# New durations in the mixer's planner, and a rule for TensorE: six projection products before a turn to small ones

## The chip, the cores and the metric

The kernel runs on one core of a Trainium2 chip. Its engines work side by side, each through a list of instructions in a fixed order: TensorE (PE) multiplies matrices, VectorE (DVE) and ScalarE (ACT) do elementwise work and reductions, GpSimd (POOL) does elementwise work and indirect transfers, and SyncE (SP) issues most transfers. Where one engine needs what another makes, it waits for a semaphore. The metric is the device time of one launch in microseconds (us); lower is better.

## The reference, cut to what matters

One residual block of 512 tokens and 1024 features: a LayerNorm, a token mixer, a second LayerNorm, a mixture of 32 experts and a third LayerNorm. The change touches the token mixer.

```python
h = LayerNorm_in(x)
p = h @ W_in + b_in                       # columns: u, v | q, k, v | z | a, b | gates A, B
A = gMLP spatial gating(u, v)             # 8 groups of 128 channels, blocks of 128 positions
B = gated delta rule(q, k, v, a, b)       # 8 heads, 128 x 128 state, chunked along the tokens
m = (sigmoid(gA) * (A @ W_pa) + sigmoid(gB) * (B @ W_pb)) @ W_o
h = LN1(alpha * h + m)
out = LN2(alpha * h + HierMoE(h))         # each token goes to 2 of 32 experts
...
# one head of B: a causal convolution of 4 taps and SiLU on q, k, v; q and k scaled to length 1
lmat = where(strict, beta * (k @ k.T) * decay, 0)
sol  = triangular_solve(eye + lmat, [v * beta, k * beta * exp(G)])
for chunk in chunks:                      # the state goes from chunk to chunk
    v_new = u_c - w_c @ state
    o     = q_dec @ state + (q @ k.T * decay) @ v_new
    state = state * cd + k_dec.T @ v_new
B = o * rsqrt(mean(o * o)) * norm_w * silu(z)
```

## The kernel before

The tokens stand in four tiles of 128. A projection of 128 output features over all 512 tokens (`proj`) is 24 products of 128x512 on TensorE: for each of eight slices of the 1024 input features three products, since weights and activations are split into a high and a low part of the type float32r (`mm3`, `split`). The weights of one projection, 512 KB, are loaded by SP (`chunk`, `column`); ACT then makes `hi` and DVE makes `lo`. There are two buffers of `hi` and `lo`, and two PSUM buffers `pd` that the projections write to in turn.

The mixer is recorded first and issued later. `Rec` takes the place of the engines: each call, `rec.tensor.matmul(...)` for instance, becomes an `Op` with the engine, the operands, a `rank` and a cost. `Rec.order` then plays the engines through in a list schedule: it takes the engine that can start something first, and on it the ready operation of lowest rank (that recorded first, where ranks are equal). The order that comes out is the order of the instructions on every engine, since they are issued in it under a manual schedule. `Rec.cost` gives two numbers in ns: how long the engine is taken, and how long after that (before) the result is there for others. Nothing at run time changes this order; where the estimates are off, an engine waits at the instruction that the plan has put next.

The recording is issued in three parts (`rec.emit`): first the first LayerNorm (`norm_in`), the gMLP and the decays; then the heads; then the merge with the residual. Behind these the second LayerNorm, the router and the experts stand in orders of their own, which `Rec` does not touch.

In the heads' part each head `h` has a front and a chain:

- `front(h)`, of rank 2h, projects k, q and v (rank one higher), convolves them on ACT and DVE (`conv`), transposes k (`tr4`), takes ACT's sums of squares (`sumsq`, tile `junk`), forms k times k (`pkk`), decays it to `L`, inverts blocks of 8 on DVE (`pl`, `Lb`, `U8`), writes `U` and `Uc` and transposes `Uc` to `Tc` (`pu`), then transposes q, takes its sums of squares, multiplies k with q (`paq`), and transposes v. All its small products go through one PSUM buffer with the tag `pf`, one after the other; the chain's last step, `po`, uses it too. The trace calls the tiles of this buffer `pk`.
- `chain(h)`, of rank 2h+1, doubles the inverted blocks in steps from 8 to 128 (`pz`, `pt`, `pu`, masks from DVE in between), then goes through four chunks of 128 tokens: `p1` (state times k and q), `R`, `p2`, `V`, `p4` and the new state `Sn`, `p3` and `o`. At the end it norms `o`, projects z, transposes `o` (`po`) and splits the product to `yh` and `yl`. Its products of blocks use a part of the array only (`128*32`, `128*64`, `64*64` in the trace).

The chain of head h and the front of head h+1 are recorded side by side, so the projections of the next head lie between the small products of this one. The gates' projections (`gates_b`) fill up: two before the first chain, six beside the last. The merge's first projection (`psi<-yh,hi` in the trace) multiplies all heads' `yh` and `yl`, the last head's at the end.

In the trace, projection products read `hi` or `lo` and write `psi`; all recorded operations have the line L215, where `issue` gives them out, so they are told apart by their tiles.

Of the kernel before, what the change touches and what calls it, by code (L numbers as in the profile page):

```python
# [16 lines left out]
F32 = mybir.dt.float32  # L17
F32R = mybir.dt.float32r
# [4 lines left out]
OP = mybir.AluOpType  # L23
# [3 lines left out]
DRAM = bass.MemoryType.DRAM  # L27
# [51 lines left out]
class Rec:  # L79
# [12 lines left out]
    def add(self, attr, eng, name, args, kw):  # L92
        op = Op(eng, name, args, kw)
        op.attr, op.rank = attr, self.rank
        op.after = self.after if eng in self.after_on else None
        aps = [(k not in self.OUTS and not (i == 0 and "out" not in kw), x)
               for i, (k, x) in enumerate([(None, x) for x in args] + list(kw.items()))
               if isinstance(x, (bass.AP, Lazy))]
        op.uses = [(read, x.tensor.name) + self.hull(x) for read, x in aps]
        op.out = [x for read, x in aps if not read][0]  # L100
        self.psum.update(x.tensor.name for _, x in aps if isinstance(x, bass.AP) and x.space == PSUM)
        op.cost, op.late = self.cost(op)
        self.ops.append(op)
        return op
# [10 lines left out]
    def cost(self, op):  # L115

        n = 1
        for x in list(op.args) + list(op.kw.values()):
            if isinstance(x, (bass.AP, Lazy)):
                m = 1  # L120
                for d in list(x.ap)[1:]:
                    m *= d[1]
                n = max(n, m)
        if op.name == "dma_start":
            return (1300, 2600) if op.eng == "SP" else (500, 15000 if op.rank else 5000)
        if op.eng == "PE":
            if op.name == "transpose":
                return 110, 200
            rhs = op.args[2]
            n = 1  # L130
            for d in list(rhs.ap)[1:]:
                n *= d[1]
            if rhs.dtype in (F32R, BF):
                return 233, 20
            m = op.args[1].shape[-1]
            if m < 128:
                return (0.55 if m == 32 else 0.9) * n, 200
            return max(224, 1.75 * n), 200
        if op.eng == "DVE":
            if op.name == "tensor_reduce":  # L140
                return 150 + 2.0 * n, 33
            if op.name == "bn_stats":
                return 640, 33
            if n == 256 and len(op.out.shape) == 4 and op.out.shape[-1] == 8:
                return 1270, 33
            if op.name == "tensor_scalar" and n == 128 and op.out.dtype == F32 and isinstance(op.args[2], bass.AP):
                return 390, 33
            return 150 + (1.15 if op.name in ("scalar_tensor_tensor", "tensor_sub") else 1.06) * n, 33
        if op.eng == "ACT":
            if op.name == "activation" and n == 128 and isinstance(op.kw.get("scale"), bass.AP):  # L150
                return 405, 33
            return (485 if "accum_out" in op.kw else 170 + 0.87 * n), 33
        return (1010 if n < 16 else 250 + 2.25 * n), 33

    def order(self):
        ops = self.ops
        last = {}
        for i, op in enumerate(ops):
            op.i, op.deps, op.outs = i, set() if op.after is None else {op.after.i}, []
            for read, name, a, b in op.uses:  # L160
                log = last.setdefault(name, [])
                for j, r, a2, b2 in log:
                    if j != i and (a < b2 and a2 < b and not (read and r) or
                                   name in self.psum and "PE" not in (op.eng, ops[j].eng) and op.eng != ops[j].eng):
                        op.deps.add(j)
                if not read:
                    log[:] = [e for e in log if not (a <= e[2] and e[3] <= b) or e[0] == i]
                log.append((i, read, a, b))
            for j in op.deps:
                ops[j].outs.append(i)  # L170
        need = [len(op.deps) for op in ops]
        ready = [0.0] * len(ops)
        free = {}
        waiting = {}
        for op in ops:
            free.setdefault(op.eng, 0.0)
            waiting.setdefault(op.eng, [])
            if not need[op.i]:
                waiting[op.eng].append(op)
        out = []  # L180
        while len(out) < len(ops):
            best = None
            for e, w in waiting.items():
                if w:
                    t = max(free[e], min(ready[o.i] for o in w))
                    if best is None or t < best[0]:
                        best = t, e
            t, e = best
            w = waiting[e]
            op = min((o for o in w if ready[o.i] <= t), key=lambda o: (o.rank, o.i))  # L190
            w.remove(op)
            op.t = t
            free[e] = t + op.cost
            out.append(op)
            for j in op.outs:
                o = ops[j]
                lat = op.late
                if op.name != "dma_start":
                    lat = 0 if o.eng == e else max(lat, 150) if o.eng == "PE" else lat
                ready[j] = max(ready[j], t + op.cost + lat)  # L200
                need[j] -= 1
                if not need[j]:
                    waiting[o.eng].append(o)
        return out
# [1781 lines left out]
```

## Time and profile before

| | |
|---|---|
| median of the runs | 1206.45 us (1206.35 to 1207.39) |
| the profiled execution | 1204.72 us |
| its span, from the first to the last instruction | 1202.9 us |
| PE busy | 1045.7 us (87% of the span), 6866 products |
| DVE busy | 656.7 us (55%) |
| ACT busy | 401.1 us (33%) |
| POOL busy | 230.7 us (19%) |
| mean granted clock of TensorE | 0.938 |

Busy times are sums over stages with different limits. The mixer takes the first part of the span; in the experts' part the weights of the experts, 1024 KB for each load, take the DMA engines. The ends of TensorE's products are modelled in the profile, so consecutive products overlap in it; the distance from start to start is what one costs. A releaser in brackets (`<-ACT junk`) names the engine and tile whose semaphore ended an idle time.

### The profile page before, as it was taken

The page shows a single profiled execution, that of the slowest core. Times are in us where ns is not written, and L with a number is a line of the kernel's source. Part 1 is how long each engine was busy: PE and PEld are TensorE (multiplying, and loading weights), DVE is VectorE, ACT ScalarE, POOL GpSimd, SP SyncE. Part 2 cuts the span into 40 slices and gives each one's busy share as a digit, 9 for nine tenths or more (in the row PEclk, how much of TensorE's full clock was granted, in tenths as well). Part 3 has the DMA queues.
Part 4 walks back from the last instruction along what each step waited for, and adds up shares of the span by engine and source line. Part 5 has one row for each costly group of instructions (what it writes and reads, how often), then busy time and mean ns, then how long its engine had stood idle before and what let it go on. Part 6 is the DMA issues. An engine that isn't in the chain of part 4 may idle for free. (4 is left out here: it accounts for less than half of the span.)

```text
span 1202.9 us, 18914 instructions
## 1 busy us (share of the span) xinstructions
PE 1045.7 (87%) x6866; PEld 687.0 (57%) x6866; DVE 656.7 (55%) x1392; ACT 401.1 (33%) x849; POOL 230.7 (19%) x296
## 2 busy tenths in 40 slices
PE   3999999999999999999999968888888879767853
PEld 2788688867777777767788633443443334333321
DVE  7566535367586777764485645453333323335584
ACT  6333337335545445444533121121111101122210
POOL 1000100022212322230100123232222212233301
PEclk8999999999999999999999979999989989876767
DMA  4422342621122111111647579999999999987996
GB/s 174 162 70 72 119 144 88 214 84 53 54 70 71 53 53 54 53 54 61 223 159 297 210 287 385 387 401 397 393 399 399 380 408 413 409 328 302 409 407 241
DMA packets 57930, 268.82 MB, mean 223 GB/s; under 512 B 12881, under 2 KB 17265, under 8 KB 33736
## 3 DMA queue, kind: packets, MB, share of 16 engines
q1 hardware_dynamic: 44400, 246.96, 53.8%
q0 software_dynamic: 10224, 10.88, 3.0%
q10 hardware_dynamic: 3176, 9.20, 2.1%
q8 instruction: 87, 1.43, 0.5%
q14 instruction: 43, 0.35, 0.1%
HBM read 274.23 MB, written 27.29 MB: 251 GB/s over the span
## 5 line engine op out<-in xcount | busy, mean ns | idle before, releaser
L215 PE MATMUL psi<-hTh,lo 128*128 128x512 f32 x448 | 183.7, 411 | 1.6 <-DVE lo L215 1.6
L215 PE MATMUL psi<-hTh,hi 128*128 128x512 f32 x448 | 184.2, 414 | 0.9 <-ACT hi L215 0.5
L215 PE MATMUL psi<-hTl,hi 128*128 128x512 f32 x448 | 183.9, 413 | 0.0
L1547 DVE TENSOR_TENSOR h<-h,u 128x640 f32<-128x640 f32 x32 | 26.3, 821 | 245.4 <-ACT h L1546 245.4
L215 DVE TENSOR_TENSOR lo<-raw,hi 128x1024 fp32r<-128x1024 f32 x74 | 92.4, 1249 | 79.8 <-ACT hi L215 79.6
L215 ACT CAST hi<-raw 128x1024 fp32r<-128x1024 f32 x74 | 77.4, 1046 | 108.0 <-PE psi L215 91.1
L1539 PE MATMUL u<-raw,xs 128*32 128x256 f32 x1120 | 79.9, 427 | 30.4 <-DMA raw<-in_w 28.7
L215 PEld LDWEIGHTS psi<-hTh,lo 128*128 128x128 f32 x448 | 84.9, 190 | 21.4 <-issue 3.9
L215 PEld LDWEIGHTS psi<-hTh,hi 128*128 128x128 f32 x448 | 85.1, 190 | 20.2 <-issue 2.6
L215 PEld LDWEIGHTS psi<-hTl,hi 128*128 128x128 f32 x448 | 84.7, 189 | 17.5 <-issue 2.0
L1546 ACT ACTIVATE h<-u 128x640 f32<-128x640 f32 x32 | 22.5, 704 | 200.8 <-PEq L1481 151.9
L1539 PE MATMUL u<-raw,x 128*64 128x512 f32 x352 | 80.8, 608 | 2.5 <-PEq L1479 1.4
L1539 PEld LDWEIGHTS u<-raw,xs 128*32 128x32 f32 x1120 | 37.9, 120 | 65.7 <-DMA raw<-in_w 37.6
L1574 POOL DMA_INDIRECT y_rows<-ysmall,itail x28 | 26.1, 933 | 223.1 <-DVE ysmall L1594 205.9
L1556 ACT COPY hT<-t 128x128 f32<-128x128 f32 x32 | 8.5, 266 | 176.4 <-PE t L1553 176.4
L1574 POOL DMA_INDIRECT y_rows<-ylarge,islot x56 | 57.2, 1022 | 44.4 <-ACT ylarge L1599 31.0
L215 DVE SCALAR_TENSOR_TENSOR acc<-xp,cols,acc 128x512 f32<-128x512 f32 x72 | 54.5, 758 | 5.3 <-ACT acc L215 4.1
L1567 PE MATMUL yz<-raw,hT 128*32 128x256 f32 x560 | 44.7, 459 | 14.3 <-DMA raw<-in_w 5.5
L1539 PEld LDWEIGHTS u<-raw,x 128*64 128x64 f32 x352 | 28.4, 140 | 49.3 <-issue 46.2
L1594 DVE COPY ysmall<-yz 32x256 f32<-32x256 f32 x112 | 46.7, 417 | 6.6 <-PE yz L1567 4.1
L1567 PE MATMUL y<-raw,hT 128*64 128x512 f32 x168 | 39.0, 604 | 7.2 <-PEq L1479 6.9
L1514 PE MATMUL t<-ident,mh 64*128 64x64 f32 x256 | 24.4, 243 | 23.5 <-PEq L1481 19.1
(505 smaller groups left out, 1987.6 us busy)
## 6 DMA issues: line engine op xcount, KB each, us to landing
raw<-in_w SPq DMA_DIRECT2D x144, 1024.0 KB
raw<-in_wt SPq DMA_DIRECT2D x73, 512.0 KB
rawl<-in_w SPq DMA_DIRECT2D x24, 1024.0 KB
rawh<-in_w SPq DMA_DIRECT2D x24, 1024.0 KB
raw<-in_wv SPq DMA_DIRECT2D x8, 512.0 KB
y_rows<-zero SPq DMA_DIRECT2D x8, 512.0 KB
raw<-y_rows ACTq DMA_DIRECT2D x4, 1024.0 KB
rawl<-in_wo SPq DMA_DIRECT2D x3, 1024.0 KB
```

The costliest lines, as they stand in the source:

```text
L215: op._ins = getattr(getattr(self.nc, op.attr), op.name)(*map(real, op.args), **{k: real(x) for k, x in op.kw.items()})
L1514: nc.tensor.transpose(self.t[0][:, k * NA:k * NA + NA], r[0][:, k * 128:k * 128 + 128], ident[0:NA, 0:NA])
L1539: self.nc.tensor.matmul(self.u[q * r:(q + 1) * r, NP if p is None else p, 0:c], x[:, k, r0:r0 + r], self.raw[b, k // 2][:, o:o + c], start ...
L1546: self.nc.scalar.activation(out=h, in_=u[:, :, 0], func=AF.Silu)
L1547: self.nc.vector.tensor_mul(out=h, in0=h, in1=u[:, :, 1])
L1556: self.nc.scalar.copy(out=x[:, n], in_=self.t[1][:, 0:128])
L1567: self.nc.tensor.matmul(y[q * r:(q + 1) * r, 0:c], t[:, i, j * r:(j + 1) * r], self.raw[b, 4 + k // 2][:, o:o + c], start=k == 0, stop=k == 3)
L1574: x = self.nc.gpsimd.indirect_dma_start(out=out, out_offset=bass.IndirectOffsetOnAxis(ap=idx, axis=0), in_=src, in_offset=None, bounds_che ...
L1594: nc.vector.tensor_copy(out=small[:, q], in_=src)
```

## The change

The diff does three things, all in `Rec`.

1. `cost` gets a new table. For DVE, ACT and POOL it gives the time for which the engine is taken and the time from the start to the result, apart from each other; a small POOL operation that is no power falls from 1010 ns to 205, a product of 128x128 is put at 180 ns taken and 386 to its result, one in 32 columns at 60 and 300, and a projection product at 232 and 394 (233 and 20 behind that, before). A transfer's time from its issue to its landing stays the same sum.
2. `order` counts a result's time from the start of its operation, with 60 ns more if another engine uses it, and 30 ns more on the same engine, where a TensorE operation follows its predecessor at once.
3. On TensorE, `order` tells projection products (`wide`, operands of type float32r) from all others. It stays with the kind that it is at, as long as one of that kind is ready; from projection products it may turn to the others once six in a row are out, and then it stays with these until none is ready. Each turn is charged in the plan, 80 ns to the small ones and 120 ns back.

No operation is added or taken away, and no buffer, rank or transfer is changed.

```diff
--- before.py
+++ after.py
@@ -99,6 +99,7 @@
         op.uses = [(read, x.tensor.name) + self.hull(x) for read, x in aps]
         op.out = [x for read, x in aps if not read][0]
         self.psum.update(x.tensor.name for _, x in aps if isinstance(x, bass.AP) and x.space == PSUM)
+        op.wide = False
         op.cost, op.late = self.cost(op)
         self.ops.append(op)
         return op
@@ -122,35 +123,44 @@
                     m *= d[1]
                 n = max(n, m)
         if op.name == "dma_start":
-            return (1300, 2600) if op.eng == "SP" else (500, 15000 if op.rank else 5000)
+            return (1300, 3900) if op.eng == "SP" else (500, 15500 if op.rank else 5500)
+        column = any(isinstance(x, bass.AP) and x.space != DRAM and x.shape[-1] == 1
+                     for x in list(op.args[2:]) + [op.kw.get(k) for k in ("bias", "scale")])
         if op.eng == "PE":
             if op.name == "transpose":
-                return 110, 200
-            rhs = op.args[2]
+                return (109, 273) if op.args[1].shape[0] == 128 else (65, 216)
+            rhs, m = op.args[2], op.args[1].shape[-1]
             n = 1
             for d in list(rhs.ap)[1:]:
                 n *= d[1]
+            op.wide = rhs.dtype == F32R
             if rhs.dtype in (F32R, BF):
-                return 233, 20
-            m = op.args[1].shape[-1]
+                return 232, 394
             if m < 128:
-                return (0.55 if m == 32 else 0.9) * n, 200
-            return max(224, 1.75 * n), 200
+                return (max(60, 0.45 * n), 300) if m == 32 else (112, 278)
+            return max(180, 0.95 * n), max(386, 2.3 * n)
         if op.eng == "DVE":
             if op.name == "tensor_reduce":
-                return 150 + 2.0 * n, 33
-            if op.name == "bn_stats":
-                return 640, 33
-            if n == 256 and len(op.out.shape) == 4 and op.out.shape[-1] == 8:
-                return 1270, 33
-            if op.name == "tensor_scalar" and n == 128 and op.out.dtype == F32 and isinstance(op.args[2], bass.AP):
-                return 390, 33
-            return 150 + (1.15 if op.name in ("scalar_tensor_tensor", "tensor_sub") else 1.06) * n, 33
+                d = 145 + 2.0 * n
+            elif op.name == "bn_stats":
+                d = 684
+            elif op.name == "tensor_scalar" and n == 128 and op.out.dtype == F32 and column:
+                d = 400
+            elif op.name == "scalar_tensor_tensor":
+                d = 185 + 1.1 * n
+            else:
+                d = 145 + 1.06 * n
+            return max(60, d - 85), d
         if op.eng == "ACT":
-            if op.name == "activation" and n == 128 and isinstance(op.kw.get("scale"), bass.AP):
-                return 405, 33
-            return (485 if "accum_out" in op.kw else 170 + 0.87 * n), 33
-        return (1010 if n < 16 else 250 + 2.25 * n), 33
+            if "accum_out" in op.kw:
+                return 400, 430
+            d = 150 + 0.875 * n + (85 if column else 0)
+            return d - 85, d
+        if n < 16:
+            d = 1010 if any(x is OP.pow for x in op.kw.values()) else 205
+        else:
+            d = 200 + (0.7 if op.name == "tensor_copy" else 1.85) * n
+        return d + 80, d
 
     def order(self):
         ops = self.ops
@@ -177,7 +187,7 @@
             waiting.setdefault(op.eng, [])
             if not need[op.i]:
                 waiting[op.eng].append(op)
-        out = []
+        out, wide, run = [], None, 0
         while len(out) < len(ops):
             best = None
             for e, w in waiting.items():
@@ -187,17 +197,27 @@
                         best = t, e
             t, e = best
             w = waiting[e]
-            op = min((o for o in w if ready[o.i] <= t), key=lambda o: (o.rank, o.i))
+            some = [o for o in w if ready[o.i] <= t]
+            if e == "PE":
+                stay = [o for o in some if o.wide == wide]
+                if stay and (not wide or run < 6):
+                    some = stay
+            op = min(some, key=lambda o: (o.rank, o.i))
             w.remove(op)
+            if e == "PE":
+                if op.wide != wide and wide is not None:
+                    t += 120 if op.wide else 80
+                wide, run = op.wide, run + 1 if op.wide == wide else 1
             op.t = t
             free[e] = t + op.cost
             out.append(op)
             for j in op.outs:
                 o = ops[j]
-                lat = op.late
-                if op.name != "dma_start":
-                    lat = 0 if o.eng == e else max(lat, 150) if o.eng == "PE" else lat
-                ready[j] = max(ready[j], t + op.cost + lat)
+                if op.name == "dma_start" or o.eng != e:
+                    lat = op.late + (0 if op.name == "dma_start" else 60)
+                else:
+                    lat = op.cost if e == "PE" else op.late + 30
+                ready[j] = max(ready[j], t + lat)
                 need[j] -= 1
                 if not need[j]:
                     waiting[o.eng].append(o)
```

## The prediction

> **What bounds the kernel now.** I read the span first, then the busy time by stage, then who waited for whom on TensorE (PE), then TensorE's own order at two places. The change acts only on the mixer, whose order a planner in the kernel writes out; so the question is what TensorE loses there.
>
> ```profile
> span 1202.9 us, 18914 instructions
> ```
>
> The table by stage has the columns stretch, length, then busy us (and instructions) of PE, PE's weight load, DVE, ACT, POOL, the granted clock, the DMA share and GB/s.
>
> ```profile
> 0.00:36.00 36.00, 17.28 (x52) 11.32 (x53) 26.75 (x78) 23.84 (x39) 4.17 (x17) 0.81 0.54 193
> 36.00:236.00 200.00, 199.35 (x912) 159.35 (x911) 101.92 (x183) 80.74 (x143) 8.26 (x17) 1.00 0.35 114
> 236.00:520.00 284.00, 277.46 (x1696) 208.49 (x1694) 202.98 (x454) 139.26 (x375) 70.78 (x109) 1.00 0.20 63
> 520.00:560.00 40.00, 37.53 (x221) 27.20 (x222) 23.98 (x60) 15.15 (x43) 7.79 (x10) 0.96 0.17 53
> 560.00:676.00 116.00, 114.39 (x541) 91.01 (x540) 74.38 (x131) 45.50 (x64) 8.37 (x8) 1.00 0.52 192
> 676.00:1202.90 526.90, 399.70 (x3449) 189.60 (x3447) 226.65 (x490) 96.62 (x190) 131.34 (x135) 0.87 0.95 373
> ```
>
> Up to 676 us TensorE is the bound: it stands idle for 0.65 us between 36 and 236, for 6.5 us between 236 and 520 (the eight heads' chains), for 2.5 us up to 560, and for 1.6 us up to 676. Behind that the experts' weights bound the kernel (DMA share 0.95). Their stream begins when the mixer's memory is given back, so a mixer that ends earlier moves the rest with it; I take that at one to one. In the first 36 us TensorE idles 18.7 us, because the first LayerNorm feeds it.
>
> Busy time is not work, though. A batch that waits for its neighbour spreads out without showing as idle. The waits of PE between 236 and 572 us (total, times, longest):
>
> ```profile
> PE pk L215 <- ACT junk L215: 3.2, 12, 0.5
> PE psi L215 <- DVE lo L215: 1.6, 3, 1.2
> PE p L215 <- ACT V L215: 1.2, 2, 1.0
> ```
>
> **The change part by part.** First I need the price of a small product. In these rows of TensorE's order (start, modelled duration), `psi` are projection products of 512 columns and `pk`, `pt` are small ones; one fp32 product makes two records, a transposition makes one.
>
> ```profile
> 341.23 0.40 PE L215 MATMUL psi<-hTh,lo 128*128 128x512 f32 x1
> 341.46 0.39 PE L215 MATMUL psi<-hTl,hi 128*128 128x512 f32 x1
> 341.69 0.27 PE L215 MATMUL pk<-ident,qT 128*128 128x128 f32 x1
> 341.72 0.48 PE L215 MATMUL psi<-hTh,hi 128*128 128x512 f32 x1
> 342.04 0.39 PE L215 MATMUL psi<-hTh,lo 128*128 128x512 f32 x1
> ...
> 343.13 0.47 PE L215 MATMUL psi<-hTh,hi 128*128 128x512 f32 x1
> 343.44 0.38 PE L215 MATMUL pk<-qT,kT 128*128 128x128 f32 x2
> 343.58 0.48 PE L215 MATMUL psi<-hTh,lo 128*128 128x512 f32 x1
> 343.90 0.40 PE L215 MATMUL psi<-hTl,hi 128*128 128x512 f32 x1
> 344.23 0.43 PE L215 MATMUL pt<-Z,Tc 128*32 128x128 f32 x8
> 344.58 0.50 PE L215 MATMUL psi<-hTh,hi 128*128 128x512 f32 x1
> 344.92 0.39 PE L215 MATMUL psi<-hTh,lo 128*128 128x512 f32 x1
> ```
>
> Two projection products in a row start 0.23 us apart (341.23, 341.46). With one transposition between them, 341.46 to 342.04 is 0.58, which is two projections and 0.11. With one product between, 343.13 to 343.58 is 0.45, which is one projection and 0.22. So turning to a full-array small product and back costs only the product. A batch of eight records of the 32-column form costs more: 343.90 to 344.92 is 1.02, less two projections 0.55. The changed planner charges 0.08 and 0.12 us for every turn, and fewer turns would seem a gain by themselves; by these rows they are none for full-array products. I put the saving by fewer turns at 0.
>
> *The batch that gets entangled.* The four products of `kT` with `qT` (`paq`) share their PSUM buffer with the four sums of squares that ACT takes of q (`junk`). One head's pass:
>
> ```profile
> 388.54 0.40 PE L215 MATMUL psi<-hTh,lo 128*128 128x512 f32 x1
> 388.77 0.38 PE L215 MATMUL pk<-qT,kT 128*128 128x128 f32 x2
> 388.91 0.48 PE L215 MATMUL psi<-hTl,hi 128*128 128x512 f32 x1
> 389.61 0.49 PE L215 MATMUL pk<-qT,kT 128*128 128x128 f32 x2 [0.22 <-ACT junk L215]
> 389.94 0.27 PE L215 MATMUL pt<-ident,Uc 128*128 128x128 f32 x1
> 389.96 0.48 PE L215 MATMUL psi<-hTh,hi 128*128 128x512 f32 x1
> 390.56 0.49 PE L215 MATMUL pk<-qT,kT 128*128 128x128 f32 x2
> 390.98 0.41 PE L215 MATMUL pz<-U,B 128*32 128x128 f32 x2
> 391.31 0.49 PE L215 MATMUL pk<-qT,kT 128*128 128x128 f32 x2
> 391.73 0.42 PE L215 MATMUL pz<-U,B 128*32 128x128 f32 x6
> 392.08 0.50 PE L215 MATMUL psi<-hTh,lo 128*128 128x512 f32 x1
> ```
>
> From 388.54 to 392.08 is 3.54 us for three projections, four `paq`, one transposition and eight tiled records. Unentangled that is 3 x 0.23 + 4 x 0.22 + 0.11 + 0.55 = 2.23, so 1.3 us is lost. The new rule sends TensorE off for six projections (6 x 0.23 = 1.4 us) after the transposition that feeds the sums of squares. In the new cost table the four sums take 4 x 0.40; at the next turn at least three of them, and by the end of the third `paq` the fourth, are done, so that the four products go out together. Twelve waits at two a head are six heads: 6 x 1.3 = 7.8 us. Bounds: 0, if ACT is late and they stay entangled; 10.4, if all eight heads have it. I take 7.8, since the wait row is of this very thing.
>
> *Tiled batches cut in two.* Here `pz` went out as 2 and 6 records, at 0.33 (390.98 to 391.31) and 0.35: a part costs about as much as a whole, 0.33 extra. Going through TensorE's order I count seven cut batches, two of which lie inside the passes above. "Does all ready ones" comes behind a longer run, when the whole batch is ready more often. Five x 0.33 = 1.7; bounds 0 and 1.7; I take half, 0.8.
>
> *Other waits.* A small product now goes up to 1.4 us after its inputs are ready, where the old plan sent it at once. That covers waits such as the 1.0 us for `V`. Of the 9.0 us idle between 236 and 560, 3.2 are the `junk` waits already counted and 2.1 are weights that come late (`lo` and its `hi`); 3.7 are left. I take half, 1.8; bounds 0 and 3.7.
>
> *The late weights.* This is the longest stop in the heads:
>
> ```profile
> 531.45 0.50 PE L215 MATMUL psi<-hTh,hi 128*128 128x512 f32 x1 [0.46 <-ACT hi L215]
> 533.13 0.50 PE L215 MATMUL psi<-hTh,lo 128*128 128x512 f32 x1 [1.18 <-DVE lo L215]
> ```
>
> The SP queue's price sums to the same 3.9 us in the plan as before, so the loads themselves don't move, and the split of the weights still waits for the projection two before. It may go away or come back at another head: I take 0, bounds 1.6 either way. The granted clock is 0.96 in 520 to 560, which is 4% of 40 us, another 1.6 us behind this stop. [...]
>
> *The price of waiting for six.* TensorE loses nothing while projections are there. The chain, however, has about 20 turns in a row for each head, and each can wait 0 to 1.4 us, 0.7 on average: 14 us longer. It is hidden behind the next head's projections (96 a head, 22 us), and for the last head behind the gates' projections:
>
> ```profile
> 571.60 0.66 PE L215 MATMUL pk<-ident,o 128*128 128x128 f32 x4
> ...
> 584.00 0.39 PE L215 MATMUL psi<-yh,hi 128*128 128x512 f32 x1
> ```
>
> Between the last head's last step and the merge's first product lie 12.4 us of other projections, and the merge needs that head only behind 21 products (4.9 us). That is 17.3 against 14 us and some 3 for scaling and splitting: just covered. Cost 0, bounds 0 and 5. With the cover gone each further us counts in full.
>
> *The start.* The transpositions of the first LayerNorm now also wait for six products where projections are ready. ACT and DVE, not TensorE, set the pace there (23.8 and 26.8 of 36 us). I take +1, bounds -2 and +3. The stretch 36 to 236 and the merge have nothing to win: 0.
>
> *What moves on the other engines.* DVE's, ACT's and POOL's orders are planned anew. POOL's small products that are no power stand at 0.285 us instead of 1.04 in the plan, three of them ahead of `L` in each head, so DVE's `L` is planned about 2.3 us sooner (an estimate from the two tables). TensorE is the bound, so this only gives slack: 0. No DMA is added; SP and ACT queues issue the same transfers.
>
> **Sum.** -7.8 - 0.8 - 1.8 + 0 + 0 + 1 = -9.4 us. The profiled execution took 1204.72 us (the span and 1.8 around it), so 1195.3 for it. The median of the runs is 1.7 higher, so 1197.0.
>
> **The rivals.**
> *Slower: the heads' own sequence becomes the bound.* The front's small products of all heads go through one PSUM buffer (`pf`) in a fixed sequence: transpositions of k, `pkk`, `pl`, `pu`, q, `paq`, v, and then the chain's `po`: eight turns a head. With 0.7 us at each that sequence grows by 5.6 us; less 1.3 for the entangled pass and 2.3 for the sooner `L`, 2.0 a head. The mechanism decides once the sequence is longer than TensorE's work for a head. For it: 6.5 us idle in 284 says that TensorE is barely the bound, so the slack may be small. Against it: projections can run up to a head ahead, and when they run out TensorE turns at once. If the first head is covered by that lead: 7 x 2.0 = 14, with the start's 1: 1206.45 + 15 = 1221. With half of it hidden, 1214.
> *No change: the gain is given back.* The entangled passes go, but the longer chain or new late weights take about as much: 1206 (within 0.2%, 2.4 us, which is about what can be told from no change).
> *All of it goes.* The 9.0 us idle, the hidden part of the passes (7.8 - 3.2 = 4.6), the cuts (1.7), the clock (1.6) and 2 at the start: 18.9, so 1187.5.
>
> **How the numbers follow.** Forecast 0.53 (own range 1191 to 1203), all of it 0.09, no change 0.14, slower 0.24. So faster by over 0.2% 0.62, same 0.14, slower 0.24. The range that leaves out no more than 2 in 10 reaches from all waits gone to the slower rival half hidden and a bit: 1186 to 1217. The time is that of the likeliest case, 1197.0.
>
> **What the profile of the changed kernel would show.** The waits of `pk` for `junk` fall from 3.2 us to under 1, and the four `paq` stand in one batch of eight records. TensorE idles under 6 us from the first head to the merge, and the merge's first product starts near 575 instead of 584. Runs of one to three projections between small products become runs of six and more. The prediction is wrong if TensorE's idle time in the heads grows, if it waits for `L`, `Uc` or `z` on DVE or for `hi` and `lo`, if the merge waits for the last head, or if the merge starts earlier and the experts' first weights do not.

## The result and the profile after

| | before | after |
|---|---|---|
| median of the runs | 1206.40 us (1206.34 to 1207.39) | 1197.38 us (1196.71 to 1198.98) |
| the profiled execution | 1204.72 us | 1196.71 us |
| its span | 1202.9 us | 1194.9 us |
| ratio of the runs, with its 95% interval | | 0.9923 (0.9908 to 0.9938) |

The change makes the kernel 0.8% faster, 9 us. The forecast was 1197.0 us. The span of the changed kernel, and its table by stage in the columns of the one before:

```profile
span 1194.9 us, 18903 instructions
```

```profile
0.00:36.00 36.00, 18.61 (x61) 13.27 (x62) 29.75 (x111) 22.94 (x39) 6.58 (x20) 1.00 0.58 210
36.00:236.00 200.00, 199.74 (x914) 159.53 (x913) 96.52 (x152) 82.75 (x150) 9.61 (x14) 1.00 0.36 115
236.00:520.00 284.00, 280.18 (x1718) 216.81 (x1717) 205.67 (x469) 139.82 (x377) 74.01 (x117) 0.99 0.19 62
520.00:560.00 40.00, 39.54 (x242) 30.65 (x241) 21.01 (x51) 17.20 (x46) 2.01 (x2) 1.00 0.21 67
560.00:676.00 116.00, 115.14 (x560) 91.41 (x558) 77.16 (x150) 41.87 (x52) 8.04 (x8) 1.00 0.59 223
676.00:1194.90 518.90, 391.37 (x3379) 181.97 (x3377) 219.85 (x463) 94.70 (x187) 132.10 (x135) 0.86 0.95 370
```

From 236 to 560 us TensorE now idles 3.8 + 0.5 = 4.3 us instead of 9.0, and more of its products fit into the same stretches (1718 and 242 instead of 1696 and 221). All of that lies in the heads; from 36 to 236 us and behind 560 the rows stay nearly as they were. The first row's clock column cannot be set beside that of before: this trace has no clock record ahead of 32.5 us, and a stretch without one reads as 1.00 (more on this in the last section). The waits of PE between 236 and 572 us (total, times, longest):

```profile
PE pk L235 <- DVE Le L235: 1.0, 3, 0.4
PE p L235 <- DVE Sn L235: 0.8, 2, 0.6
PE p L235 <- ACT U L235: 0.7, 1, 0.7
PE p L235 <- ACT V L235: 0.4, 1, 0.4
...
PE psi L235 <- DVE lo L235: 0.2, 1, 0.2
```

The row for `junk`, the largest before, is gone, and so is most of the wait for `lo` (a second execution of this kernel, from another session, has 0.8 us of it). What is left is spread over the heads' own tiles, none over 1.0 us in all. One head's pass that was entangled before, now in TensorE's order:

```profile
379.57 0.39 PE L235 MATMUL psi<-hTl,hi 128*128 128x512 f32 x1
379.80 0.83 PE L235 MATMUL pk<-qT,kT 128*128 128x128 f32 x6
380.46 0.27 PE L235 MATMUL pt<-ident,Uc 128*128 128x128 f32 x1
380.67 0.43 PE L235 MATMUL pz<-U,B 128*32 128x128 f32 x8
381.02 0.50 PE L235 MATMUL psi<-hTh,hi 128*128 128x512 f32 x1
...
382.29 0.39 PE L235 MATMUL psi<-hTl,hi 128*128 128x512 f32 x1
382.52 0.38 PE L235 MATMUL pk<-qT,kT 128*128 128x128 f32 x2
382.66 0.48 PE L235 MATMUL psi<-hTh,hi 128*128 128x512 f32 x1
```

Three of the four `paq` products go out in one batch of six records, the transposition and an uncut `pz` behind them; then come six projections, then the fourth product. From 379.57 to 381.02 is 1.45 us for one projection, three products, one transposition and eight tiled records; by the prediction's prices that is 0.23 + 0.66 + 0.11 + 0.55 = 1.55. So nothing is lost in this pass any more. By the same prices, from a head's first `paq` product to the record behind its last, the eight passes lost 8.2 us before (1.1 to 1.4 in six heads, 0.7 and nothing in the other two) and lose 1.3 now. The 32 `paq` products, 32 single turns before, stand in 16 batches: all four together, as was forecast, in two heads, three and one in four heads, two and two singles in the other two. Between 236 and 560 us there were 211 runs of projections, and now there are 133, of which 118 are of exactly six.

The end of the heads, the last head's last transposition and the merge's first product:

```profile
567.47 0.60 PE L235 MATMUL pk<-ident,o 128*128 128x128 f32 x4
...
572.58 0.39 PE L235 MATMUL psi<-yh,hi 128*128 128x512 f32 x1
```

The merge starts at 572.6 instead of 584.0. Only 5 us of other projections are left between the two, where there were 12.4: the last head's chain did become longer (from its `Uc` to its last step 42.9 us instead of 33.0).

Marks on the way, in us from the span's start, read from the same places of each trace:

| | before | after | gained so far | gained in the part |
|---|---|---|---|---|
| first transposition of k (heads begin) | 235.3 | 233.2 | 2.1 | start 2.1 |
| merge's first product | 584.0 | 572.6 | 11.4 | heads 9.3 |
| merge's last product | 630.1 | 617.2 | 12.9 | merge 1.5 |
| last product of the output projection (`po`) | 687.3 | 674.3 | 13.0 | 0.1 |
| span's end | 1202.9 | 1194.9 | 8.0 | experts -5.0 |

The last row is the puzzle: 13 us gained up to the output projection, 8 at the end.

### The profile page after: what moved, and what is told of

Its sections match the earlier page's. It is cut to its first block, busy times and chain, and to the rows that moved or that the text cites. A ratio compares the mean times of both kernels' runs of the same rounds, so it can differ in the third digit from the quotient of the medians.

```text
span 1194.9 us, 18903 instructions
## 1 busy us (share of the span) xinstructions
PE 1044.6 (87%) x6866; PEld 693.6 (58%) x6866; DVE 650.0 (54%) x1392; ACT 399.3 (33%) x849; POOL 232.4 (19%) x296
## 5 line engine op out<-in xcount | busy, mean ns | idle before, releaser
L235 PE MATMUL psi<-hTl,hi 128*128 128x512 f32 x448 | 177.8, 399 | 0.0
L1559 PE MATMUL u<-raw,xs 128*32 128x256 f32 x1120 | 77.1, 417 | 24.2 <-DMA raw<-in_w 22.7
L235 PEld LDWEIGHTS psi<-hTh,lo 128*128 128x128 f32 x448 | 84.9, 190 | 18.7 <-issue 2.1
L235 PEld LDWEIGHTS psi<-hTl,hi 128*128 128x128 f32 x448 | 84.8, 189 | 18.7 <-issue 1.3
L1587 PE MATMUL y<-raw,hT 128*64 128x512 f32 x168 | 42.5, 641 | 5.7 <-PEq L1499 3.6
```

The costliest lines, as they stand in the source:

```text
L235: op._ins = getattr(getattr(self.nc, op.attr), op.name)(*map(real, op.args), **{k: real(x) for k, x in op.kw.items()})
L1559: self.nc.tensor.matmul(self.u[q * r:(q + 1) * r, NP if p is None else p, 0:c], x[:, k, r0:r0 + r], self.raw[b, k // 2][:, o:o + c], start ...
L1587: self.nc.tensor.matmul(y[q * r:(q + 1) * r, 0:c], t[:, i, j * r:(j + 1) * r], self.raw[b, 4 + k // 2][:, o:o + c], start=k == 0, stop=k == 3)
```

## The experiments

The table of durations, the rule on TensorE and their working together were taken apart; the forecast's two largest claims (the entangled batch, and the heads' own sequence as the rival bound) were tried by themselves; and the end was delayed to see what the experts' part passes on. Times are medians, ratios are to the kernel before in the same session; there were two sessions.

**The new table alone.**

```diff
-                stay = [o for o in some if o.wide == wide]
-                if stay and (not wide or run < 6):
-                    some = stay
...
-                if op.wide != wide and wide is not None:
-                    t += 120 if op.wide else 80
```

> The new table and the new way of counting results, without the rule of six and without the charge for a turn. Theory A (the rule unties the products of k and q from ACT's sums of squares): the table alone leaves these products one by one among the sums, so the waits of pk for junk stay near 3 us and the heads gain at most 2 us; with 2 us at the start and 1.5 in the merge the kernel comes to 1202 to 1205. Theory B (the better durations make the gain, the rule adds little): waits fall under 1.5 us, 1197 to 1200.

Measured: 1199.83 us, 0.9953 (0.9935 to 0.9971). By the ratios that is 5.7 us (3.5 to 7.8) of the change's 9.3 (7.5 to 11.1). The time is that of the second expectation, the waits and batches are those of the first. Its waits of PE between 236 and 572:

```profile
PE pk L231 <- ACT junk L231: 2.7, 11, 0.4
PE pt L231 <- DVE U L231: 1.9, 1, 1.9
...
PE psi L231 <- DVE lo L231: 0.2, 1, 0.2
```

The `junk` waits stay (all 32 `paq` are still single turns); it is the wait for `lo` that falls, from 1.6 us to 0.2. The heads take 346.2 us instead of 348.7, so within the heads the table alone gives 2.5 us of the change's 9.3, and the passes of `paq` still lose 7.4. The heads begin 2.1 us earlier.

**The rule alone,** with its charges, on the old table.

```diff
+        op.wide = eng == "PE" and name == "matmul" and args[2].dtype == F32R
...
+                stay = [o for o in some if o.wide == wide]
+                if stay and (not wide or run < 6):
+                    some = stay
```

> The old table with the rule of six and its charge. Theory A: the products of k and q go out in two batches a head, waits of pk for junk under 1 us, the heads gain 7 to 9.5 us, the start and the merge nothing: 1198 to 1201. Theory B: TensorE turns at times that the old table has wrong, and waits move to other tiles: 1203 to 1207.

Measured: 1206.64 us, 1.0010 (0.9995 to 1.0024): no gain, so the theory of a gain by the rule alone (1198 to 1201) falls and the other's time holds. Its waits, and the stretch in which the weights come late:

```profile
PE pk L225 <- ACT junk L225: 3.4, 7, 0.5
PE psi L225 <- DVE lo L225: 2.0, 4, 1.0
PE pz L225 <- DVE U L225: 1.4, 2, 1.0
```

```profile
520.00:560.00 40.00, 36.72 (x225) 27.16 (x225) 21.65 (x55) 14.24 (x41) 5.69 (x10) 0.91 0.15 52
```

Here `paq` stands in 15 batches, much as in the changed kernel, and its passes lose 3.4 us instead of 8.2. The wait for `junk` is as long as before, but 2.0 us of it now stand ahead of the transpositions of k and 1.4 at `paq`, where there were 1.9. So the rule does untie the products, and yet the heads are no shorter (348.6 us instead of 348.7). Part of what takes the gain back can be seen: TensorE idles 10.0 us between 236 and 560 instead of 9.0, late weights among it, and its clock is at half for 6.8 us instead of 3.4 (0.91 from 520 to 560 us, 0.96 before). The rest isn't placed. The rule needs the table. Which entry of the table it needs wasn't tried.

**The entangled batch alone.** The kernel before, in which the four `paq` are planned behind all four sums of squares:

```diff
+        was, nc.after = (nc.after, nc.after_on), sums
+        nc.after_on = ("PE",)
         for j in range(4):
             te.matmul(paq[:, j], kT[:, j], qT[:, j], start=True, stop=True)
```

> The kernel before, with one thing done: the four products of k and q are planned behind all four sums of squares of q, as one batch. Theory A prices this at 6 heads x 1.3 us = 7.8: the heads end 6 to 8 us sooner, the kernel takes 1198.5 to 1200.5. Theory C (the lost time in these passes is only moved, other waits of the fronts and chains take it up): the heads end at most 3 us sooner, 1203.5 to 1206.5.

Measured: 1201.08 us, 0.9964 (0.9950 to 0.9978), between the two expectations. One such pass:

```profile
388.48 0.41 PE L215 MATMUL pz<-U,B 128*32 128x128 f32 x2
388.82 1.16 PE L215 MATMUL pk<-qT,kT 128*128 128x128 f32 x8
389.91 0.42 PE L215 MATMUL pz<-U,B 128*32 128x128 f32 x6
```

The four products go out at once and still cut a `pz` batch in two (0.34 and 0.35 us for the parts). The heads take 5.5 us less (343.1 instead of 348.7). The passes of `paq` by themselves lose 0.4 us instead of 8.2, so untying them is worth 7.8 there, as the prediction had it. The heads gain less, since other waits grow: TensorE idles 9.3 us between 236 and 560, as much as before, though the 1.9 us at `paq` are gone. The largest of them is a new stop of 2.1 us, once, for `hi`:

```profile
PE psi L215 <- ACT hi L215: 2.1, 1, 2.1
PE pz L215 <- DVE U L215: 1.5, 2, 0.9
PE pk L215 <- ACT junk L215: 1.5, 3, 0.5
```

**The table and the entangled batch, without the rule,** run in both sessions.

> The new table without the rule of six and its charge, and the four products of k and q planned behind all four sums of squares. Theory D (the two parts of the change work together only because the rule unties these products and the table places everything else): the heads' 4.6 us of the table and 5.5 of the untied products add up to about 10, 1196 to 1199, as the full change. Theory E (the rule's slack of up to 1.4 us before each small product takes up waits that this does not): 1198.5 to 1201.5, with waits for U, V, R and Sn left in the heads.

> The version with the new table and the paq edit, without the rule and its charge, as measured before at 1192.95 us (0.9884). If it beats the changed kernel: 1190 to 1195, 2 to 6 us under the changed kernel on the same chip. If that was the chance of one batch: 1196 to 1199.

Measured: 1192.95 us, 0.9884 (0.9867 to 0.9901), the first time, which is below both expectations. The second session's kernels, the one before among them, all took about 1% longer, which in the changed kernel lies behind the output projection (below), so from there only ratios are used: 0.9892 (0.9861 to 0.9923), and for the changed kernel itself beside it 0.9890:

> The changed kernel itself, for a comparison with the two versions beside it on the same chip: 1196 to 1199 us.

In the first session this version was 4.4 us under the changed kernel, in the second 1.0 us (1206.10 and 1207.12) with equal ratios. So the 2 to 6 us that were to be seen again were not. Its mixer does end a little earlier, at 673.3 and 672.9 us against 674.3 and 675.4, so 1 to 2.5 us are likely; a faster kernel isn't shown. What is shown is that it is at least as fast without the rule. The two parts also do more together than apart: its heads take 336.7 us, 12.0 less than before, where the table alone gave 2.5 and the batch alone 5.5.

```profile
236.00:520.00 284.00, 281.10 (x1739) 213.38 (x1738) 207.55 (x484) 141.62 (x385) 73.33 (x117) 1.00 0.18 63
```

```profile
PE psi L231 <- ACT z L231: 1.1, 1, 1.1
PE psi L231 <- DVE lo L231: 0.6, 2, 0.3
```

TensorE idles 2.9 us in the heads' main stretch, and the last head's chain is done at 555.6 us, 12.2 before the changed kernel's.

**The change and the entangled batch together.**

> The changed kernel with one thing more: the four products of kT with qT are planned behind all four sums of squares. Theory E (rule and paq edit serve the same end, and the rule adds slack of its own): at least as fast as the version with the new table and the paq edit but no rule, 1189 to 1193 us. Theory F (with the entangled batch gone the rule has nothing left to win, and its runs of six only lengthen the last chain): slower than that version, about as the change itself, 1194 to 1199 us, and the last head's final transposition over 3 us later than there (555.6 us).

Measured: 0.9908 (0.9881 to 0.9936), 1208.2 us beside 1206.1 without the rule and 1207.1 for the change. The intervals overlap widely; neither theory is told from the other by the time. The second half of F shows: the last head's transposition stands at 571.1 instead of 555.0. That costs nothing, since the merge starts at 571.7 and ends 0.9 us behind the version without the rule. With the batch untied by hand no gain of the rule is left to be seen.

**Six, three, nine, twelve.** One number of the rule:

```diff
-                if stay and (not wide or run < 6):
+                if stay and (not wide or run < 12):
```

> The changed kernel with three projection products before a turn in place of six. Theory E (slack): a wait of 0.7 us at most before a small product covers less, the products of k and q fall apart again into more batches, 1199 to 1203. Theory D: 1197 to 1200. If the last chain's length mattered, it would be some 5 us shorter here (10 us longer than before with six) and the time lower: 1194 to 1196.

> The changed kernel with nine projection products instead of six before a turn. 9 x 0.23 = 2.1 us a run, 1.0 us mean wait at a turn instead of 0.7. If the heads' own sequence becomes the bound at once behind six: between the changed kernel and the run of twelve (1197 and 1244), so about 1210 to 1225, with PE idle over 10 us between 236 and 560. If the cover lasts up to nine: 1195 to 1202.

> The changed kernel with twelve projection products before a turn. The prediction's rival (the heads' own sequence becomes the bound when each turn waits): each turn waits up to 2.8 us, 1.4 on average, eight turns a head make the fronts 5.6 us a head longer than with six and twenty turns make the last chain 14 us longer, which the gates' projections no longer cover: 1210 to 1235. If TensorE stays the bound whatever the turns wait: 1195 to 1200.

| projections before a turn | ratio to before | merge's first product | last head's last step | PE idle 236 to 560 |
|---|---|---|---|---|
| 3 | 1.0028 (1.0016 to 1.0039) | 586.4 | 568.5 | 11.7 |
| 6 | 0.9923 (0.9908 to 0.9938) | 572.6 | 567.8 | 4.3 |
| 9 (second session; 6 there: 0.9890) | 1.0047 (1.0020 to 1.0073) | 582.6 | 588.5 | 13.4 |
| 12 | 1.0310 (1.0292 to 1.0327) | 609.7 | 622.2 | 25.6 |

Twelve took 1243.67 us, more than the 1210 to 1235 expected for it. At nine and twelve the last head ends behind the merge's first product, and TensorE waits for the heads. First nine:

```profile
PE pt L235 <- DVE U L235: 4.8, 3, 4.0
PE p L235 <- ACT V L235: 1.4, 4, 0.4
```

```profile
520.00:560.00 40.00, 32.59 (x193) 23.66 (x194) 21.56 (x56) 15.06 (x46) 8.44 (x15) 0.91 0.13 40
```

Then twelve:

```profile
PE pt L235 <- DVE U L235: 6.5, 2, 4.0
PE pz L235 <- DVE Z L235: 2.7, 1, 2.7
```

```profile
236.00:520.00 284.00, 269.65 (x1565) 209.23 (x1564) 186.38 (x410) 125.51 (x327) 62.87 (x102) 0.96 0.18 60
520.00:560.00 40.00, 28.79 (x182) 21.25 (x180) 24.41 (x78) 14.61 (x55) 9.52 (x16) 0.81 0.01 5
```

That is the forecast's slower rival: the heads' own sequence takes over, projections run out, and TensorE stands idle for whole microseconds. At nine it decides at the last head: up to 520 us TensorE idles 6.0 us, no more than before (6.5), and the stop of 4.0 us stands at 535.1, at the last head's first doubling step. At twelve it shows in every stretch. Three is slower than no rule at all with the same table (1.0028 against 0.9953), outside of all that I expected. Its waits:

```profile
PE pz L235 <- DVE U L235: 2.3, 4, 0.9
PE pk L235 <- DVE L L235: 1.9, 1, 1.9
PE pk L235 <- ACT junk L235: 1.5, 6, 0.5
```

The longest wait is 1.9 us, and 15 of its 23 `paq` turns are single products. Three loses 12 us against six (13.3 in the heads by the marks), and the trace places most of it: TensorE idles 11.7 us instead of 4.3, the passes of `paq` lose 6.0 instead of 1.3, and 13 batches of the 32-column form are cut in two instead of 2, at 0.33 us each 3.6 us more. These overlap in part, and on the other side the clock never falls in its heads (1.00 from 236 to 520 and from 520 to 560 us). Why the plan with three comes out that way isn't settled.

**The heads' part alone** planned anew, the start and the merge with the old costs and in the old order.

```diff
+    rec.old = True
...
+    rec.old = False
...
+    rec.old = True
...
-        for op in self.order():
+        for op in (self.order_old if self.old else self.order)():
```

> The changed planner for the heads alone; the first part (LayerNorm, gMLP, decays) and the merge are planned as before. If the 2.1 us that the start and the 1.5 us that the merge were shorter come from the new plan and pass on to the end: 1200 to 1202. If the start's share is only a clock window that fell otherwise in that execution, or is lost again further on: 1197 to 1199.

Measured: 1197.14 us, 0.9930 (0.9908 to 0.9951), the same as the whole change and as the second expectation. The heads take 339.8 us, as in the changed kernel (339.4). Its merge takes 44.5 us in the old order, and in every other kernel of the study whose last head is in time 44.4 to 45.7; the 46.1 us of before hold one wait of 1.3 us for `lo`, which of the others only the version with the table and `paq` has (0.8 and 1.1). So the "1.5 us gained in the merge" of the table of marks do not come from a new plan of the merge.

**Later by 22 us.** The changed kernel with four projections more at the end of the heads, whose results nobody reads (4 x 24 x 0.23 = 22 us):

```diff
+    for i in range(4, 8):
+        kk.proj(57 + i)
```

> The changed kernel with four more projections at the end of the heads whose results nothing reads (96 products of 0.233 us, 22.4 us of TensorE time), so that everything behind them begins later. If the experts' part moves with its start, as the prediction took it: 1218 to 1221. If it absorbs a part, as the profiled executions suggest (12.9 us sooner at its start, 8.0 at the end): 0.6 to 0.7 of 22.4, 1211 to 1214.

Measured: 1216.05 us, 1.0084 (1.0068 to 1.0101), 18.7 us over the changed kernel (16 to 21 by the intervals). That is between the two expectations. In its trace the last product of the output projection comes 20.6 us later (694.9) and not 22.4; the clock, at half for 3.4 us in its heads and for 6.8 in the changed kernel's, accounts for 1.7 of the difference by an estimate (half of the 3.4 us between them). So 0.9 of what the mixer lost arrives at the end; against these 20.6, one to one is within the interval.

All nine kernels of the first session can be read the same way. The change of the time (ratio times 1206.4), less the change of the output projection's last product, is +0.6 us for the table alone, +2.2 rule, +3.5 `paq`, +1.9 heads, +3.7 the change, 0.0 table and `paq`, +2.7 three, +1.0 twelve, +2.5 later: +2.0 on average, with no trend, whether the mixer ends 14 us earlier or 36 later. A loss that grew with the gain would not look so; a common offset points to the one execution of before that all are compared with. From that mark to the end the traced executions of the session took 515.5 to 522.3 us; the 515.6 of before are near the short end, the 520.6 of the changed kernel near the middle of the rest.

## Why the prediction was right, and where not

- **The bound** was read rightly: the gain lies on TensorE in the heads, 9.3 us by the marks, where the terms for the heads (7.8 + 0.8 + 1.8) make 10.4.
- **The entangled batch, -7.8:** right in mechanism and close in size, 6.9 us by the prediction's own prices (8.2 before, 1.3 after). One step of its sizing held by luck: of the twelve `junk` waits taken as two a head, nine stand at `paq` and three at the transpositions of k and q; the nine still fall on six heads. Neither of the two reasons given does it alone: the table leaves 7.4 us in the passes, and the rule leaves 3.4 but the heads keep their length.
- **Cut batches, -0.8:** of the 32-column batches seven were cut before, as counted, and two are now, but of the `128*64` batches one was cut before and five are now. Eight against seven is little won; what a cut of the second form costs wasn't measured.
- **Other waits, -1.8:** not borne out. What is left of the idle time without `junk` and the weights was 3.7 us and is about 4 now: `V` fell from 1.2 to 0.4, but `Le` and `U` came in its place. The gain came from what the prediction had not counted on: the weights, next, and the three `junk` waits outside the passes (1.3 us).
- **The late weights, 0, and the other engines' new order, "only gives slack: 0":** both too low. The stops for `lo` and `hi` fell from 2.1 us to 0.2 (0.8 in the second execution), and the table alone takes most of them away and shortens the heads by 2.5 us with all `paq` turns still single. The likely way, not shown by a run of its own, is that better durations on DVE and ACT move the split of the weights, for which TensorE waits.
- **The start, +1:** wrong in sign by the marks. Over the kernels that plan the start with the new table the heads begin 1.9 us earlier on average (1.0 to 2.6). Part of the 2.1 us of the changed kernel's trace is the clock: its projection products start 0.43 us apart up to 32.1 us and 0.23 apart from 32.8, where the kernel before reads 0.50 up to 35.8; half speed for the 3.3 us from 32.5 to 35.8 is up to 1.6 us, an estimate. Whether the new plan makes it rise sooner isn't shown. The rule on the old table begins the heads 0.6 us later, the sign that was forecast, though within the scatter of single executions. At the end none of this can be seen: the heads alone give the same time.
- **The merge, 0:** right (see the heads' part alone).
- **Waiting for six, 0:** right, with less to spare than thought. The last chain became 10 us longer where 14 were priced, and the cover shrank from 12.4 + 4.9 to 5.1 + 4.9 us. At nine it is used up.
- **Experts one to one:** borne out within the noise by the later end (18.7 of 20.6 us) and by the offsets without a trend. That the 5 us which the experts' part takes longer in the one traced execution are scatter is argued from these, not shown.
- **The sum:** by the marks the mixer gained 12.9 us where the terms made 9.4. The heads gave 9.3 where 10.4 were forecast, the start 2.1 where a loss of 1 was, the merge 1.5 where nothing was. The median gained 9. That the two agree is in part luck: terms that gave less were made up by terms put at nothing, and some 2 us of the 12.9 are the common offset above. I put that down to the one execution of before; it is argued, not shown, and what is left lies within the scatter of the offsets (0.0 to 3.7).
- **The slower rival** was a real mechanism. It decides between six and nine.
- **What the profile would show:** `junk` under 1 us (none), idle under 6 us (4.3 from 236 to 560, and no new wait up to the merge), the merge near 575 (572.6), runs of six (118 of 133): as said. Eight records in one batch: in two heads of eight.

## What to carry over

Try the durations of a list schedule and its rule apart: here the new durations alone gave 5.7 us of 9.3 by the medians (2.5 of 9.3 within the heads), while the rule on the old ones gave nothing, though it did untie the products that it was made for. In this kernel six was the best of the four values tried, with time lost at three and at nine, and the cover on the long side (here the work between the last chain and its user) can be read from the trace beforehand. Where one exchange between two engines is the suspect, order that exchange by hand: with the new table, planning four products behind four sums gave at least as much as the general rule did. And size a removed loss by what it frees and by what the stretch gains: of the 7.8 us of the untied passes 5.5 were left when other waits had grown.

## What the runs showed of the hardware

TensorE's clock fell in the changed kernel's heads without a stop longer than a microsecond. It reads 0.50 for 6.8 us, about 3.4 us of loss by that figure, right behind the stretch that holds the longest of the waits above, the 0.7 us for `U`; in a second execution and in the heads-alone kernel it falls near the same place (0.68 from 274 to 282 us, and 0.75 from 274.9 to 281.7). PE busy, then the other engines as in the stage table, the clock third from the end:

```profile
271.50:274.90 3.40, 2.66 (x24) 1.81 (x23) 2.44 (x6) 2.53 (x6) 2.89 (x6) 1.00 0.00 0
274.90:281.70 6.80, 6.55 (x18) 4.84 (x18) 5.23 (x19) 2.79 (x8) 2.53 (x3) 0.50 0.23 77
```

TensorE was busy for 2.66 of the 3.4 us ahead of it, 78%. Neither a longer stop nor a lower busy share brought such a fall by itself: the run of three, at its stop of 1.9 us, is busy for 1.65 of 3.4 us, less than half, and reads 1.00 behind it:

```profile
326.60:330.00 3.40, 1.65 (x8) 1.41 (x9) 1.97 (x5) 0.63 (x1) 1.50 (x5) 1.00 0.02 5
330.00:333.40 3.40, 3.40 (x17) 2.66 (x16) 2.80 (x6) 1.90 (x3) 3.09 (x4) 1.00 0.00 0
```

The stretch ahead of the fall held mostly `64*64` products and two projection products at most, this one six projections; whether that is what counts wasn't tried.

The clock column needs care at the start of a trace. It reads 0.81 for the first 36 us of before and 1.00 for the same plan in the version with `paq` alone, but that trace has no clock record ahead of 34.0 us. Just ahead of that its projection products start 0.42 us apart, as those of before do up to 35.4, and 0.23 apart behind it. The first two rows are from before, the others from `paq` alone:

```profile
34.50 0.63 PE L215 MATMUL pv<-yal,hTh 128*128 128x512 f32 x1
34.92 0.63 PE L215 MATMUL pv<-yah,hTl 128*128 128x512 f32 x1
```

```profile
33.27 0.63 PE L215 MATMUL pv<-yal,hTh 128*128 128x512 f32 x1
33.69 0.54 PE L215 MATMUL pv<-yah,hTl 128*128 128x512 f32 x1
```

The clock column of before reads 0.50 from 28.0 to 35.4 us. So by the spacing both were at half speed, and what differs is when the clock rose. With the same plan of the start the heads began at 234.5, 235.3 and 235.6 us in three kernels (`paq`, before, heads alone), so a first mark can be off by 1 us without the kernel's doing. And the experts' part took 10 us longer in the second session at the same work, while the mixer kept its time (last product of the changed kernel's output projection at 674.3 and 675.4, spans of 1194.9 and 1206.6).

So a difference of 1% between sessions lay here almost wholly in a stage that the change doesn't touch (10.6 of the 11.7 us between the two spans), and only ratios from one session can be set beside each other.
